# Hybrid decoder block: parameter loads as rows, and the gates of the second token block made when that block begins

## The chip, the cores and the metric

One core of a Trainium2 chip runs the whole program. The metric is the device time of one execution in microseconds (us). The kernel before took 3391.08 us (median of 3 runs, 3389.36 to 3392.07).

## The reference, cut to what matters

A block of 2048 tokens and 1024 channels: two branches in parallel, merged with gates, and then a dense part.

```
h = rms(x);  u, q, k, v, qi, ki, wi, gates = split(h @ w_in)
y_ssm = s5(u, A_re, A_im, log_dt, B, C, D_skip, ...)   # state space scan, gelu, glu
y_att = dsa(q, k, v, qi, ki, wi)                       # the best 256 keys of each query, then softmax
g_ssm, g_att = split(gates)                            # 2 x 1024 columns
merged = sigmoid(g_ssm) * (y_ssm @ w_proj_ssm) + sigmoid(g_att) * (y_att @ w_proj_attn)
x = x + merged @ w_out
x = x + (silu(h2 @ w_gate) * (h2 @ w_up)) @ w_down     # h2 = rms(x), 2816 columns inside
```

All in float32. The matrix products are each made as three products of parts (high by high, high by low, low by high), which the code calls mm3.

## The kernel before, in words

**Who sets the order.** The kernel writes one order of instructions for each engine. It is made by a planner (class Pace) that keeps an estimated clock of each engine: generators yield what they wait for, and the first in the list that is ready by TensorE's estimated clock goes on. The list is state space branch, attention, dense part; so the dense part fills what the two others leave free. All loads and stores are issued by SyncE (SP) in one queue, in order.

**Phase 1** (names tp, mm, hT, w, raw) norms x, transposes it into hT and multiplies it with the columns of w_in for keys, queries and u. The state space parameters are prepared beside it (`ssm_params`): its loads and small VectorE operations are put into a queue, `small`, of which `drain` takes up to 8 after each tile of q or u. In the queue all loads stand first: A_re, A_im, log_dt and D_skip are read straight into a layout with state and group on the partitions, in pieces of one element; B_re and B_im in pieces of 16 elements.

**Gates** (`gates`, names gps, gw, gsg): 16 column tiles of 128 for each half of the tokens, the second half first. Each weight tile is loaded raw and split into a high and a low part by GpSimd (POOL), VectorE (DVE) or ScalarE (ACT); a gate is 24 matmuls of 512 columns, a tanh on ACT, and a store. For the first half, hT is read back from the tensor hTd, which phase 1 stores. Tokens 0 to 511 are block 0 of the dense part, tokens 512 to 1023 block 1.

**Attention** goes over four groups of four query tiles. Each has scores of the indexer (tps), a search of the thresholds (`topk`: counting on DVE, names jkd, tr, un, cnt, and on ACT, jka), and then the attention itself (lg, pt, po). The search needs little of TensorE.

**Dense part** (`block`, PSUM name f) for four token blocks of 512: merge (f<-act,ww, one load of a gate tile and one product on DVE for each bank), w_out (f<-ww,mg), norm, and the feed-forward: up and gate (f<-h,ww) and down (f<-wd,at, where each 6 matmuls end in one addition x<-f,x on DVE). In block 0 each weight is loaded raw, split, and its parts stored (wc<-ww); the later blocks load the parts. Block 0 begins when the glu of the state space branch is done (name u) and the gates are; each later block when the attention of its group is.

Of the kernel before, what the change touches and what calls it, by code (L numbers as in the profile page):

```python
# [25 lines left out]
KD = D // 128  # L26
# [25 lines left out]
class Pace:  # L52
# [95 lines left out]
    def at(self, eng, *what):  # L148

        return lambda: self.when(eng, what) + (None,)  # L150
# [215 lines left out]
class Block:  # L366
    def __init__(self, ctx, tc, a, out):
        self.tc, self.a, self.out = tc, a, out
        self.pace = self.nc = nc = Pace(tc.nc)
        self.const = self.pool(ctx, "const", 1)  # L370
        self.attended, self.act, self.gated, self.exps = 0, [], False, False
        self.spare_banks, self.lent = 0, False
        self.dram = ctx.enter_context(tc.tile_pool(name="scr", bufs=1, space=DRAM))
        c = self.const
        self.ident = c.tile([128, 128], F32, name="ident")
        make_identity(tc.nc, self.ident)
        self.mhalf = c.tile([128, 64], F32, name="mhalf")
# [12 lines left out]
        self.u_d = [d.tile([128, G, TC, PG], F32, name=f"u{i}") for i in range(2)]  # L390
        self.hT_d = d.tile([128, 2, KD, HALF], F32, name="hTd")
        self.bias_d = [d.tile([128, (i + 1) * 128], BF16, name=f"bias{i}") for i in range(NT)]
        self.gate_d = [[d.tile([128, HALF], F32, name=f"gate{j}_{h}") for h in range(2)] for j in range(2 * KD)]
        self.y_d = [[d.tile([64, HALF], F32, name=f"y{i}_{h}") for h in range(2)] for i in range(8)]
        self.act_d, self.att_d = ([d.tile([128, 2, 4, TB], F32, name=f"{n}{i}") for i in range(NB)]
                                  for n in ("act", "att"))
# [338 lines left out]
    def gates(self, hT, st):  # L735
# [21 lines left out]
            yield  # L757
        psp = self.pool(st, "gps", 2, PSUM)
        NG = 2 * KD
        order = [(n, tg) for n in range(2 * NG) for tg in range(2)]  # L760

        order[2 * NG - 4:2 * NG + 4] = [(NG + n, tg) for n0 in (-2, 0) for tg in range(2) for n in (n0, n0 + 1)]
        there = [[0.0, 0.0], [0.0, 0.0]]
        parts = deque()

# [7 lines left out]
        left = [2] * (2 * NG)  # L773
        for q, (n, tg) in enumerate(order):
            hf, ct = 1 - n // NG, n % NG
            ld.need(2 * n + 2)
            ld.allowed = 2 * sum(z == 0 for z in left) + 4
            left[n] -= 1
            w = tiles[n]
            sl = slice(tg * 512, (tg + 1) * 512)  # L780
            while parts and parts[0][0] == tg:
                reload()
            yield self.pace.at("PE", w, there[tg][0], psp.free_at("gps"))
            if q in (2 * NG - 2, 2 * NG):
                parts.extend((q - 2 * NG + 2 >> 1, h, i) for h in range(2) for i in range(2))
# [444 lines left out]
    def ssm_params(self, pr, wk, ps_t, queue):  # L1230

        nc, a = self.nc, self.a
        NS = G // 2
        dv, sync, cmul = Later(queue, nc.vector), Later(queue, nc.sync), self.cmul
        sh = [128, NS]
        A = {}
        for n in ("A_re", "A_im"):
            A[n] = wk.tile(sh, F32, name=n)
            ap = a[n]
            sync.dma_start(A[n], bass.AP(tensor=ap.tensor, offset=ap.offset, ap=[[1, 128], [128, NS]]))  # L1240
        dt = wk.tile(sh, F32, name="dt")
        ap = a["log_dt"]
        for g2 in range(2):
            sync.dma_start(dt[g2 * 64:(g2 + 1) * 64],
                              bass.AP(tensor=ap.tensor, offset=ap.offset + g2, ap=[[0, 64], [2, NS]]))
        Ds = pr.tile([32, NS], F32, name="Ds")
        ap = a["D_skip"]
        sync.dma_start(Ds, bass.AP(tensor=ap.tensor, offset=ap.offset, ap=[[1, 32], [32, NS]]))
        B, C, turns = [], [], []
        for n in ("B_re", "B_im"):  # L1250
            t = wk.tile([128, NS, PG], F32, name=n)
            ap = a[n]
            sync.dma_start(t, bass.AP(tensor=ap.tensor, offset=ap.offset,
                                         ap=[[PG, 128], [128 * PG, NS], [1, PG]]))
            B.append(t)
        for n in ("C_re", "C_im"):
            t = pr.tile([128, NS, PG], F32, name=n)
            ap = a[n]
# [14 lines left out]
        ar, ai = A["A_re"], A["A_im"]  # L1273
# [55 lines left out]
        u1, u2 = (wk.tile([128, NS, PG], F32, name=f"u{n}") for n in "12")  # L1329
# [5 lines left out]
        dv.tensor_tensor(eye, self.ident[:32, 0:PG], self.ident[:32, PG:2 * PG], op=ALU.add)  # L1335
        queue.extend(turns)
        return m8, ap_r, ap_i, wt, Bb, C, eye, Ds

# [302 lines left out]
    def weights(self):  # L1641
# [23 lines left out]
        return [(kind, parts, copy, tb > 0) for tb in range(NB) for (kind, parts), copy in zip(items, copies)]  # L1665

    def load_branch(self, bigp, br, tb):

        z = bigp.tile([128, 2, 4, TB], F32R, name=f"act{br}")
        for k in range(4):  # L1670
            self.nc.sync.dma_start(z[:, :, k].bitcast(F32), (self.act_d, self.att_d)[br][tb][:, :, k])
        return z

    def block(self, tb, bigp, ld, nps, nd):

# [7 lines left out]
        with ExitStack() as st:  # L1683
# [25 lines left out]
            def ready(*w):  # L1709
                return at("PE", free, *w)  # L1710

            with ExitStack() as sm:
                mp = self.pool(sm, "mg", 1)
                mg = mp.tile([128, 2, KD, n], F32R, name="mg")
                with ExitStack() as sp:
# [9 lines left out]
                    load_gate(0, 0)  # L1725
# [3 lines left out]
                    load_gate(1, 0)  # L1729
                    load_gate(0, 1)  # L1730
                    load_gate(1, 1)
                    for q, (ct, br) in enumerate([(0, 0), (1, 0), (0, 1), (1, 1)] +
                                                 [(ct, br) for ct in range(2, KD) for br in range(2)]):
# [9 lines left out]
                        if br == 1:  # L1743
# [172 lines left out]
                        yield from down(pairs.popleft(), False)  # L1916
                pairs.append(acts)
            if tb + 1 < NB:
                self.act = [self.load_branch(bigp, br, tb + 1) for br in range(1 + (self.attended >= 4 * (tb + 2)))]
# [83 lines left out]
```

## Time and profile before

| | |
|---|---|
| median of the runs | 3391.08 us |
| the profiled execution's own time | 3392.47 us |
| its span | 3390.8 us |
| PE busy | 3179.1 us (94%) |
| DVE busy | 2118.4 us (62%) |
| ACT, POOL busy | 1277.2 us (38%), 622.4 us (18%) |
| DMA | 605.67 MB, 51.1% of 16 engines |

Read it by stages: the shares are means over stages with different limits. A row of the timeline gives the start, the duration of a run of like instructions, the engine, and in brackets the idle time before it and what ended it. Matmuls are pipelined, so a PE that is busy all the time can still be slow: what counts is how many of them are done in a stretch.

### The profile page before, as it was taken

What the parts mean: (1) busy time and instruction counts of PE and PEld (TensorE: products, weight loads), DVE (VectorE), ACT (ScalarE), POOL (GpSimd) and SP (SyncE); (2) the same over time, 40 slices, a digit from 0 to 9 for tenths busy, and PEclk for the clock granted to TensorE, in tenths of its full rate; (3) what the DMA queues carried; (4) which work ended last, traced back from release to release, by engine and by line L of the source; (5) the groups of instructions that cost most, each with busy time, mean ns of one, the idle gap of its engine ahead of it and who ended that gap; (6) DMA issues with size and microseconds to landing.
All of it is one profiled execution on the core that took longest, in us unless ns stands there. A gap on an engine that the chain in (4) does not pass through costs nothing. (4 is left out here: it accounts for less than half of the span.)

```text
span 3390.8 us, 44218 instructions
## 1 busy us (share of the span) xinstructions
PE 3179.1 (94%) x16292; PEld 2687.4 (79%) x16292; DVE 2118.4 (62%) x4540; ACT 1277.2 (38%) x2210; POOL 622.4 (18%) x620
## 2 busy tenths in 40 slices
PE   6999999899878999988889999999999999899999
PEld 5889777677767888876788888878888888698887
DVE  5565595655687767689686675867776666322223
ACT  3141444445552444355412443666124443010000
POOL 3323666522233212134100000000000000000000
PEclk8999999999989999999999999999999999999999
DMA  4834423434458766656845324376472332755554
GB/s 135 249 119 116 132 77 121 153 123 142 130 174 293 271 210 231 238 175 236 310 152 218 146 105 165 123 259 229 166 271 99 114 133 103 271 193 201 204 199 161
DMA packets 321527, 605.67 MB, mean 179 GB/s; under 512 B 52896, under 2 KB 205216, under 8 KB 290592
## 3 DMA queue, kind: packets, MB, share of 16 engines
q1 hardware_dynamic: 321312, 602.86, 51.1%
q8 instruction: 128, 2.10, 0.2%
q14 instruction: 87, 0.71, 0.1%
HBM read 434.71 MB, written 166.89 MB: 177 GB/s over the span
## 5 line engine op out<-in xcount | busy, mean ns | idle before, releaser
L206 PE MATMUL f<-h,ww 128*128 128x512 f32 (+1 forms) x4416 | 1015.0, 384 | 1.4 <-DVE h L206 1.1
L206 PEld LDWEIGHTS f<-h,ww 128*128 128x128 f32 x4416 | 800.6, 190 | 156.4 <-DVE h L206 1.9
L206 PE MATMUL f<-wd,at 128*128 128x512 f32 x2112 | 521.1, 399 | 42.8 <-DVE un L206 16.0
L206 PEld LDWEIGHTS f<-wd,at 128*128 128x128 f32 x2112 | 398.5, 192 | 133.3 <-DVE x L206 13.6
L206 PE MATMUL gps<-hT,gw 128*128 128x512 f32 x1536 | 386.5, 402 | 5.2 <-ACT gsg L206 3.7
L206 ACT ACTIVATE jka<-S,tr 128x1536 bf16<-128x1536 f32 (+5 forms) x217 | 305.6, 1408 | 193.6 <-DVE tr L206 119.2
L206 PEld LDWEIGHTS gps<-hT,gw 128*128 128x128 f32 x1536 | 287.7, 192 | 70.0 <-ACT gsg L206 6.4
L206 DVE TENSOR_TENSOR x<-f,x 128x512 f32<-128x512 f32 x352 | 236.4, 687 | 103.2 <-PE f L206 102.5
L206 PE MATMUL mm<-w,hT 128*128 128x512 f32 (+1 forms) x1152 | 281.5, 402 | 7.2 <-DVE hT L206 7.0
L206 DVE TENSOR_TENSOR tl<-pt,th 128x512 fp32r<-128x512 f32 (+1 forms) x288 | 184.2, 658 | 135.9 <-ACT th L206 135.1
L206 PEld LDWEIGHTS mm<-w,hT 128*128 128x128 f32 x1152 | 241.8, 241 | 32.6 <-DVE hT L206 8.7
L206 DVE SCALAR_TENSOR_TENSOR t<-t,f 128x512 f32<-128x512 f32 (+1 forms) x125 | 83.5, 668 | 278.5 <-PE f L206 238.0
L206 ACT CAST th<-pt 128x512 fp32r<-128x512 f32 (+1 forms) x288 | 155.8, 563 | 234.1 <-PE pt L206 230.3
L206 PE MATMUL f<-act,ww 128*128 128x512 f32 x768 | 189.9, 408 | 29.7 <-POOL ww L206 9.1
L206 PEld LDWEIGHTS f<-act,ww 128*128 128x128 f32 x768 | 149.2, 197 | 70.3 <-POOL ww L206 13.3
L206 PE MATMUL f<-ww,mg 128*128 128x256 f32 x1536 | 190.4, 287 | 10.8 <-ACT ww L206 4.5
L206 PEld LDWEIGHTS f<-ww,mg 128*128 128x128 f32 x1536 | 188.7, 195 | 12.9 <-ACT ww L206 5.0
L206 ACT ACTIVATE P<-P,m 128x1024 f32<-128x1024 f32 (+7 forms) x192 | 172.3, 900 | 54.5 <-DVE m L206 54.4
L206 POOL TENSOR_TENSOR g<-g,g 128x512 f32<-128x512 f32 x31 | 39.8, 1285 | 813.3 <-DVE g L206 793.5
L206 PE MATMUL lg<-kk,q 128*128 128x512 f32 (+1 forms) x640 | 183.7, 388 | 1.1 <-DMA kk<-kk 1.1
L206 ACT ACTIVATE t<-f 128x512 f32<-128x512 f32 (+1 forms) x92 | 53.0, 576 | 332.9 <-PE f L206 332.7
L206 ACT CAST at<-t 128x512 fp32r<-128x512 f32 (+1 forms) x92 | 55.3, 601 | 324.1 <-DVE t L206 324.1
(359 smaller groups left out, 4492.2 us busy)
## 6 DMA issues: line engine op xcount, KB each, us to landing
ww<-wc SPq DMA_DIRECT2D x180, 1024.0 KB, 4.9
wd<-wc SPq DMA_DIRECT2D x66, 1024.0 KB, 8.3
wc<-ww SPq DMA_DIRECT2D x60, 1024.0 KB, 7.7
raw<-in_w_in_dram SPq DMA_DIRECT2D x104, 256.0 KB, 3.4
wc<-wd SPq DMA_DIRECT2D x22, 1024.0 KB, 7.6
x<-in_x_dram SPq DMA_DIRECT2D x32, 512.0 KB, 5.1
gate<-gsg SPq DMA_DIRECT2D x64, 256.0 KB, 2.2
g<-gate SPq DMA_DIRECT2D x64, 256.0 KB, 5.0
```

What stands on the lines that cost most here:

```text
L206: return f(*args, **kw)
```

## The change

Parameters: A_re, A_im, D_skip and log_dt are loaded as rows (16 partitions), four small transposes on TensorE turn them (`columns`), and ACT copies them out of PSUM. B_re and B_im are loaded in four pieces each, and the loads of B and the rest of C stand between the small operations instead of ahead of all of them. Gates: in the first half of the tokens `gates` makes only tokens 0 to 511, and stores each split weight tile (`gw_d`). Block 1 begins with 16 gate products from these stored parts and from hT, which is loaded from hTd into the buffers of the activations; its branches are loaded as those buffers come free, attention first.

```diff
+        self.late = (1,)
+        self.gw_d = [d.tile([128, 2, 1024], F32, name=f"gw{j}") for j in range(2 * KD)]
...
-        order = [(n, tg) for n in range(2 * NG) for tg in range(2)]
-
-        order[2 * NG - 4:2 * NG + 4] = [(NG + n, tg) for n0 in (-2, 0) for tg in range(2) for n in (n0, n0 + 1)]
+        order = [(n, tg) for n in range(NG) for tg in range(2)] + [(NG + n, 0) for n in range(NG)]
+
+        order[2 * NG - 4:2 * NG] = [(n, tg) for tg in range(2) for n in (NG - 2, NG - 1)]
...
-            if q in (2 * NG - 2, 2 * NG):
-                parts.extend((q - 2 * NG + 2 >> 1, h, i) for h in range(2) for i in range(2))
+            if q == 2 * NG - 2:
+                parts.extend((0, h, i) for h in range(2) for i in range(2))
+            if n >= NG:
+                nc.sync.dma_start(self.gw_d[ct], w.rearrange("p z k c -> p z (k c)").bitcast(F32))
...
+        for z, n, m in ((rows[0], "A_re", 128), (rows[1], "A_im", 128), (d32, "D_skip", 32), (d2, "log_dt", 2)):
+            sync.dma_start(z, bass.AP(tensor=a[n].tensor, offset=a[n].offset, ap=[[m, NS], [1, m]]))
...
+        def columns():
+            nc.scalar.copy(rows[2].rearrange("p (a n) -> p a n", a=2), d2[:, :, None].to_broadcast([NS, 2, NST]))
+            ps = ps_t.tile([128, 512], F32, name="tp")
+            for i, z in enumerate(rows):
+                nc.tensor.transpose(ps[:, i * NS:(i + 1) * NS], z, self.ident[:NS, :NS])
+            nc.tensor.transpose(ps[:32, 3 * NS:4 * NS], d32, self.ident[:NS, :NS])
+            nc.scalar.copy(A.rearrange("p a s -> p (a s)"), ps[:, :3 * NS])
+            nc.scalar.copy(Ds, ps[:32, 3 * NS:4 * NS])
...
-            sync.dma_start(t, bass.AP(tensor=ap.tensor, offset=ap.offset,
-                                         ap=[[PG, 128], [128 * PG, NS], [1, PG]]))
+            for s0 in range(0, NS, 4):
+                sync.dma_start(t[:, s0:s0 + 4], bass.AP(tensor=ap.tensor, offset=ap.offset + s0 * 128 * PG,
+                                                        ap=[[PG, 128], [128 * PG, 4], [1, PG]]))
...
+        queue.extend(head)
+        queue.extend(loads.popleft() for _ in range(24))
+        queue.append(columns)
+        for i, step in enumerate(steps):
+            queue.append(step)
+            if i % 6 == 5 and loads:
+                queue.append(loads.popleft())
...
+                [("w", None, copy, True) for copy in self.gw_d if tb in self.late] +
...
+                    order = list(range(KD))
+                    last = 3
+                    for ct in range(2 * KD - last):
+                        w = ld.get("w")
+                        yield ready(w, *hg)
+                        ps = bank()
+                        yield from products(ps, w, order)
+                        ld.drop("w")
+                        gated(ct, ps)
...
+                    self.act = [None, self.load_branch(bigp, 1, tb)]
+                    for i in range(last):
+                        w = ld.get("w")
+                        yield from products(banks[i], w, order[KD // 2:])
+                        ld.drop("w")
+                        gated(2 * KD - last + i, banks[i])
+                    self.act[0] = self.load_branch(bigp, 0, tb)
...
+                if tb + 1 in self.late:
+                    self.act = self.load_tokens(bigp, tb + 1)
```

The queue of SP in phase 1, from the third weight load on. Before (A, dt, Ds, B and C are the parameters, raw a weight):

```order
L206 DMA raw<-in_w_in_dram 128x512 x3
L206 DMA A_re<-in_A_re_dram 128x16x1
L206 DMA A_im<-in_A_im_dram 128x16x1
L206 DMA dt<-in_log_dt_dram 64x16x1 x2
L206 DMA Ds<-in_D_skip_dram 32x16x1
L206 DMA B_re<-in_B_re_dram 128x16x16
L206 DMA B_im<-in_B_im_dram 128x16x16
L206 DMA C_re_568<-in_C_re_dram 16x2x64
L206 DMA raw<-in_w_in_dram 128x512 x3
```

The same place now (u_577 and u_578 are buffers for the rows):

```order
L206 DMA raw<-in_w_in_dram 128x512 x3
L206 DMA u_577<-in_A_re_dram 16x128
L206 DMA u_577<-in_A_im_dram 16x128
L206 DMA u_578<-in_D_skip_dram 16x32
L206 DMA u_578<-in_log_dt_dram 16x2
L206 DMA C_re_584<-in_C_re_dram 16x2x64 x4
L206 DMA raw<-in_w_in_dram 128x512 x3
```

Between the two groups of weight loads stand eight small loads; the first pieces of B have moved behind the loads of C.

TensorE at the end of the glu (u) and the begin of block 0, before (act_9327 and act_9364 are the two branches):

```order
L206 MATMUL gps<-hT,gw 128x512 x24
L206 MATMUL u<-yp,uw_7369 128x256 x12
L206 MATMUL u<-yp,uw_7374 128x256 x12
L206 MATMUL gps<-hT,gw 128x512 x6
L206 MATMUL u<-yp,uw_7416 128x256 x12
L206 MATMUL u<-yp,uw_7443 128x256 x12
L206 MATMUL gps<-hT,gw 128x512 x330
L206 MATMUL f<-act_9327,ww 128x512 x24
```

and now:

```order
L206 MATMUL gps<-hT,gw 128x512 x24
L206 MATMUL u<-yp,uw_7424 128x256 x12
L206 MATMUL u<-yp,uw_7429 128x256 x12
L206 MATMUL u<-yp,uw_7481 128x256 x12
L206 MATMUL u<-yp,uw_7484 128x256 x12
L206 MATMUL u<-yp,uw_7424 128x256 x12
L206 MATMUL u<-yp,uw_7429 128x256 x12
L206 MATMUL u<-yp,uw_7481 128x256 x12
L206 MATMUL u<-yp,uw_7484 128x256 x12
L206 MATMUL f<-act_8639,ww 128x512 x24
```

The 330 gate matmuls between the glu and block 0 are gone, and the last 96 matmuls of the glu have no gate between them.

TensorE at the end of block 0 and the begin of block 1 now (tps is the indexer of the third group, hg the stored hT, act the branches):

```order
L206 MATMUL tps<-kis,qi 128x512 x8
L206 MATMUL f<-wd,at 128x512 x6
L206 MATMUL tps<-kis,qi 128x256 x8
L206 MATMUL f<-wd,at 128x512 x66
L206 MATMUL f<-hg_13765,ww 128x512 x12
L206 MATMUL f<-hg_13768,ww 128x512 x12
...
L206 MATMUL f<-hg_13768,ww 128x512 x48
L206 MATMUL f<-hg_13765,ww 128x512 x36
L206 MATMUL f<-act_14743,ww 128x512 x24
```

Before, 240 down and 294 up matmuls of block 0 stood between the third group's last tps and the first f<-act of block 1; now 66 down matmuls and the 384 gate matmuls stand there. Where the second group's search runs, between the last u and the first lg of that group, the order of TensorE holds 408 up matmuls of 512 columns and 144 down matmuls behind the merge, w_out and norm of block 0; before it held 330 gate matmuls ahead of them, 108 up matmuls behind, and no down. After the last lg of the program 186 more matmuls of 512 columns are left than before. On POOL, 89 splits of the dense part's weights stand where there were 69.

## Rows read from the trace of the kernel before

**Rows 1.** The page: busy tenths of TensorE in 40 slices of the span.

```profile
PE   6999999899878999988889999999999999899999
```

**Rows 2.** By stretch: length; busy PE, PEld, DVE, ACT, POOL; clock, DMA share, GB/s.

```profile
70.00:80.00 10.00, 0.00 (x0) 0.00 (x0) 0.00 (x0) 0.00 (x0) 0.00 (x0) 0.60 0.05 0
...
900.00:981.00 81.00, 77.17 (x337) 62.02 (x336) 71.76 (x263) 59.55 (x104) 17.21 (x15) 1.00 0.29 88
981.00:1163.00 182.00, 147.07 (x814) 125.87 (x815) 135.05 (x262) 55.04 (x82) 57.48 (x31) 0.90 0.79 278
1478.00:1634.00 156.00, 127.24 (x506) 100.20 (x506) 143.36 (x296) 86.93 (x111) 65.44 (x28) 0.91 0.67 237
```

**Rows 3.** Timeline of SP's issues in phase 1: start, time taken, load.

```profile
56.80 0.42 SPq L206 DMA_DIRECT2D A_re<-in_A_re_dram  x1
57.28 3.56 SPq L206 DMA_DIRECT2D A_im<-in_A_im_dram  x1
...
66.66 4.80 SPq L206 DMA_DIRECT2D B_re<-in_B_re_dram  x1
71.50 12.86 SPq L206 DMA_DIRECT2D B_im<-in_B_im_dram  x1
...
85.81 1.31 SPq L206 DMA_DIRECT2D raw<-in_w_in_dram  x3
```

**Rows 4.** Timeline of the compute engines around the same place.

```profile
61.20 1.04 PE L206 MATMUL tp<-ident,x 128*128 128x128 f32 x8
...
88.70 0.43 DVE L206 CAST w<-raw 128x512 fp32r<-128x512 f32 x1 [23.31 <-DMA raw<-in_w_in_dram]
...
91.74 1.97 PE L206 MATMUL tp<-ident,q 128*128 128x128 f32 x8 [22.15 <-DVE hT L206]
```

**Rows 5.** Timeline of TensorE between the glu and block 0.

```profile
900.66 26.44 PE L206 MATMUL gps<-hT,gw 128*128 128x512 f32 x114
928.71 22.49 PE L206 MATMUL gps<-hT,gw 128*128 128x512 f32 x96 [1.61 <-ACT gsg L206]
952.83 27.96 PE L206 MATMUL gps<-hT,gw 128*128 128x512 f32 x120 [1.64 <-ACT gsg L206]
989.65 5.43 PE L206 MATMUL f<-act,ww 128*128 128x512 f32 x12 [8.86 <-DMA act<-act]
```

**Rows 6.** Timeline of TensorE at the end of block 0, beside the third group's search.

```profile
1497.26 21.93 PE L206 MATMUL f<-h,ww 128*128 128x512 f32 x96
1519.02 1.07 PE L206 MATMUL f<-wd,at 128*128 128x512 f32 x4
...
1543.41 23.47 PE L206 MATMUL f<-h,ww 128*128 128x512 f32 x96
1566.72 1.07 PE L206 MATMUL f<-wd,at 128*128 128x512 f32 x4
...
1583.52 11.04 PE L206 MATMUL f<-h,ww 128*128 128x512 f32 x48
1594.40 1.07 PE L206 MATMUL f<-wd,at 128*128 128x512 f32 x4
...
1632.05 2.11 PE L206 MATMUL f<-act,ww 128*128 128x512 f32 x8 [1.86 <-DVE x L206]
```

**Rows 7.** Timeline of DVE at the begin of that search: the same instruction twice.

```profile
1486.52 2.38 DVE L206 SCALAR_TENSOR_TENSOR tr<-un,tr 128x1 int32<-128x1 int32 x1
...
1491.95 0.16 DVE L206 SCALAR_TENSOR_TENSOR tr<-un,tr 128x1 int32<-128x1 int32 x1
```

**Rows 8.** Groups of instructions: count, busy us, mean ns of one, idle before and releasers.

```profile
L206 DVE TENSOR_TENSOR x<-f,x 128x512 f32<-128x512 f32 x352 | 236.4, 687 | 103.2 <-PE f L206 102.5
...
L206 POOL TENSOR_TENSOR ww<-raw,ww 128x1024 fp32r<-128x1024 f32 x33 | 81.4, 2468 | 110.4 <-ACT ww L206 90.0 <-DVE m L206 7.9 <-DMA wc<-ww 7.7
...
L206 POOL TENSOR_TENSOR ww<-raw,zeros 128x1024 fp32r<-128x1024 f32 x13 | 28.3, 2174 | 79.2 <-PE f L206 38.7 <-DMA raw<-in_w_proj_attn_dram 24.1 <-DMA raw<-in_w_ffn_gate_dram 11.4
```

**Rows 9.** Timeline of TensorE where the fourth group's attention has ended and block 2 ends.

```profile
2908.60 1.62 PE L206 MATMUL f<-wd,at 128*128 128x512 f32 x3 [5.36 <-DMA wd<-wc]
```

More of the change, by code (lines that the diff above doesn't have):

```diff
@@ L771, in reload @@
                 there[tg][h] = self.pace.ready(hT)
-        left = [2] * (2 * NG)
+        left = [2] * NG + [1] * NG
         for q, (n, tg) in enumerate(order):
@@ L1233, in ssm_params @@
         NS = G // 2
-        dv, sync, cmul = Later(queue, nc.vector), Later(queue, nc.sync), self.cmul
+        head, steps, loads = [], [], deque()
+        dv, cmul = Later(steps, nc.vector), self.cmul
         sh = [128, NS]
[L1236 to L1245, printed above, removed]
-        Ds = pr.tile([32, NS], F32, name="Ds")
-        ap = a["D_skip"]
-        sync.dma_start(Ds, bass.AP(tensor=ap.tensor, offset=ap.offset, ap=[[1, 32], [32, NS]]))
+        u1, u2 = (wk.tile([128, NS, PG], F32, name=f"u{n}") for n in "12")
+        v1, v2 = (u.rearrange("p s c -> p (s c)")[:NS] for u in (u1, u2))
+        rows = [v1[:, 0:128], v1[:, 128:256], v2[:, 0:128]]
+        d32, d2 = v2[:, 128:160], v2[:, 160:162]
+        sync = Later(head, nc.sync)
+        for z, n, m in ((rows[0], "A_re", 128), (rows[1], "A_im", 128), (d32, "D_skip", 32), (d2, "log_dt", 2)):
+            sync.dma_start(z, bass.AP(tensor=a[n].tensor, offset=a[n].offset, ap=[[m, NS], [1, m]]))
+        A = wk.tile([128, 3, NS], F32, name="A")
+        Ds = pr.tile([32, NS], F32, name="Ds")
+        def columns():
[6 more added lines that the diff above has]
+            nc.scalar.copy(Ds, ps[:32, 3 * NS:4 * NS])
+        dt = A[:, 2]
+        late = []
+        sync = Later(late, nc.sync)
         B, C, turns = [], [], []
@@ L1252, in ssm_params @@
             ap = a[n]
[L1253 to L1254 removed]
+            for s0 in range(0, NS, 4):
+                sync.dma_start(t[:, s0:s0 + 4], bass.AP(tensor=ap.tensor, offset=ap.offset + s0 * 128 * PG,
+                                                        ap=[[PG, 128], [128 * PG, 4], [1, PG]]))
             B.append(t)
+        sync = Later(loads, nc.sync)
         for n in ("C_re", "C_im"):
@@ L1272, in ssm_params @@
             C.append(t)
-        ar, ai = A["A_re"], A["A_im"]
+        ar, ai = A[:, 0], A[:, 1]
         edt, _ = self.exp_parts(dv, dt, wk, sh, "ed")
@@ L1335, in ssm_params @@
         dv.tensor_tensor(eye, self.ident[:32, 0:PG], self.ident[:32, PG:2 * PG], op=ALU.add)
+        loads.extend(late)
+        queue.extend(head)
[5 more added lines that the diff above has]
+                queue.append(loads.popleft())
+        assert not loads and len(steps) > 7 * 16
         queue.extend(turns)
@@ L1664, in weights @@
         copies = [self.dram.tile([128, 2, 1024], F32, name=f"wc{i}") for i in range(len(items))]
-        return [(kind, parts, copy, tb > 0) for tb in range(NB) for (kind, parts), copy in zip(items, copies)]
+        return [z for tb in range(NB) for z in
+                [("w", None, copy, True) for copy in self.gw_d if tb in self.late] +
+                [(kind, parts, copy, tb > 0) for (kind, parts), copy in zip(items, copies)]]
     def load_branch(self, bigp, br, tb):
@@ L1672, in load_branch, with load_tokens @@
         return z
+    def load_tokens(self, bigp, tb):
+        hg = []
+        for i in range(2):
+            ks = slice(i * KD // 2, (i + 1) * KD // 2)
+            hg.append(bigp.tile([128, 2, KD // 2, TB], F32R, name=f"hg{i}", tag=f"act{i}"))
+            for z in range(2):
+                self.nc.sync.dma_start(hg[i][:, z].bitcast(F32), self.hT_d[:, z, ks, tb * TB:(tb + 1) * TB])
+        return hg
     def block(self, tb, bigp, ld, nps, nd):
@@ L1710, in ready, with products, gated @@
                 return at("PE", free, *w)
+            b0 = 0
+            if tb in self.late:
+                b0 = 1
+                with ExitStack() as sg:
+                    gp = self.pool(sg, "lsg", 2)
+                    hg = self.act
+                    def products(ps, w, ks):
+                        w = w.rearrange("p z a (k c) -> p (z a) k c", k=KD)
+                        for k in ks:
+                            z = hg[k // 4]
+                            self.mm3(ps, w[:, 0, k], w[:, 1, k], z[:, 0, k % 4], z[:, 1, k % 4], k == order[0],
+                                     k == order[-1])
+                            if k % 2 == 1:
+                                ld.tick()
+                                if k != order[-1]:
+                                    yield at("PE")
+                    def gated(ct, ps):
+                        g = gp.tile([128, n], F32, name="lg")
+                        nc.scalar.activation(g, ps, AF.Tanh, scale=0.5)
+                        nc.sync.dma_start(self.gate_d[ct][hf][:, h0:h0 + n], g)
+                    order = list(range(KD))
[7 more added lines that the diff above has]
+                        gated(ct, ps)
+                    order = [*range(KD // 2, KD), *range(KD // 2)]
+                    banks = []
+                    for i in range(last):
+                        w = ld.get("w", i)
+                        yield ready(w)
+                        banks.append(bank(False))
+                        yield from products(banks[i], w, order[:KD // 2])
+                    self.act = [None, self.load_branch(bigp, 1, tb)]
+                    for i in range(last):
+                        w = ld.get("w")
[3 more added lines that the diff above has]
+                    self.act[0] = self.load_branch(bigp, 0, tb)
             with ExitStack() as sm:
@@ L1728, in block @@
                     self.act = []
[L1729 to L1733, printed above, removed]
+                    load_gate(1, b0)
+                    load_gate(0, b1)
+                    load_gate(1, b1)
+                    for q, (ct, br) in enumerate([(0, b0), (1, b0), (0, b1), (1, b1)] +
+                                                 [(ct, br) for ct in range(2, KD) for br in (b0, b1)]):
                         w = ld.get("w", 1 if q == 1 else 0)
@@ L1918, in block @@
             if tb + 1 < NB:
-                self.act = [self.load_branch(bigp, br, tb + 1) for br in range(1 + (self.attended >= 4 * (tb + 2)))]
+                if tb + 1 in self.late:
+                    self.act = self.load_tokens(bigp, tb + 1)
+                else:
+                    self.act = [self.load_branch(bigp, br, tb + 1)
+                                for br in range(1 + (self.attended >= 4 * (tb + 2)))]
             yield from down(pairs.popleft(), False)
```

6 lines of the change are left out of this document (3 added, 3 removed).

## The prediction

> **What bounds the kernel now.** I read the busy tenths of TensorE first [rows 1]: it is busy nearly everywhere, so its work is the floor, and what can be gained is the time in which it stands or gets through few matmuls. The change neither adds nor removes products of size: 384 gate matmuls go from one place to another. So I looked for the stretches in which TensorE loses time, and asked which of them the moved work touches. Three matter.
>
> The first is in phase 1. SyncE needs 3.56 us to issue A_im and 12.86 us for B_im, against 0.42 us for A_re, which I read as the many small pieces of the loads ahead filling the queue; the next weight loads are issued only at 85.81 [rows 3]. DVE then waited 23.31 us for them, and TensorE stood for 22.15 us [rows 4]. From 70 to 80 no compute engine did anything [rows 2], so nothing was done ahead in that time.
>
> The second is where the second attention group's search runs, from the end of the glu at about 900 to 1163. First 330 gate matmuls cover it, at nearly full rate: PE is busy 77.17 of 81 us [rows 2, 5]. Then block 0 begins, and PE is busy only 147.07 of 182 us.
>
> The third is the third group's search, 1478 to 1634: 506 matmuls of 512 columns in 156 us [rows 2]. At the full rate, 21.93 us for 96 or 0.228 us for one [rows 6], they need 115.6 us, so 40 us are lost. The loss is in the down parts: every 6 matmuls wait for an addition of 0.687 us on DVE [rows 8], which is busy 143.36 of the 156 us. DVE itself is held up while POOL splits weights: the same one-element instruction takes 2.38 us there and 0.16 us a little later [rows 7].
>
> **The change, part by part.** *The parameter loads.* In place of A, dt, Ds and B stand eight loads, each of a few hundred pieces at most. At the 0.42 us of A_re [rows 3] they take 3.4 us of SyncE, so that the next weights are issued at about 60 and not at 85.81. A weight reached DVE 2.9 us after that issue (88.70 less 85.81) [rows 3, 4], so it is there at about 63, and DVE asked for it at 65.4 (88.70 less 23.31). The stall of 22.15 us goes. With it goes the slow start behind it, 1.97 us for eight transposes that took 1.04 us before [rows 4]. Against these 23 us stand four small transposes and three ACT copies, about 1 us. I take -22 us. What may be late next are the eight pieces of B: they are issued between weights later. From below, they cost nothing, since the weights are loaded ahead; from above, a quarter of B_im's 12.86 us each, 25.7 us in all, which would eat the gain.
>
> *The gates that go.* The 330 gate matmuls between the glu and block 0 took from 900.66 to 980.79, 80.1 us, for 75.3 us of work at 0.228 us. Their other 54 stood between the matmuls of the glu and filled its waits. Of the work nothing is saved; the 5 us that they lost there go: -5 us. The glu's last 96 matmuls have no filler now, which costs at most 54 times 0.228, 12 us; since without a filler in the way they can follow each other faster, I take 0.
>
> *Block 0 comes 80 us earlier and lies wholly in the second group's search.* Its start (8.86 us of waiting for the branch [rows 5]) and its merge lose what they lost before. New there are 144 down matmuls, three parts of 48, which the order now has ahead of that group's first lg. The nearest rows are the down parts in the third group's search [rows 6]: 1519.02 to 1543.41 is 24.4 us for 48, 1566.72 to 1583.52 is 16.8 us, 1594.40 to 1632.05 is 37.7 us for 96. Less 11.0 us of work for 48 that is a loss of 13.4, 5.8 and twice 7.9 us, 8.7 us in the mean: +26 us for three, from 0 if that search has ended by then to +40 at the worst part. The second cost is POOL's: 20 more splits, 2.17 or 2.47 us each [rows 8], stand on it, at most 49 us in which DVE's search may stand. DVE was busy 71.76 and 135.05 of the 263 us [rows 2], so 56 us are free, and the additions and products that come in take some 17 us of them (24 additions of 0.687 us; what the up parts bring to DVE is about what it saves in splits). The rest hides most of it; I take +7, from 0 to +49. Together +33 us.
>
> *Block 1 begins with the gates.* They need DVE for nothing: tanh on ACT, a store, and weights that are already split. In the third group's search the 240 down matmuls become 66, and no POOL split is left beside it. Of the 40 us lost I keep 66/48 of 8.7 us, 12 us. The gates themselves read 4 MB of hT and 1 MB of weights for each 24 matmuls, and then the two branches come into buffers that the gates have just left. The nearest row is the wait of 8.86 us for a branch at block 0's start [rows 5]; between 0 and twice that I take +7. So -40 + 12 + 7 = -21 us, from -40 to -4.
>
> *The tail.* With less work beside the searches at the end, the attention of the last group ends earlier: 186 more matmuls follow its last lg. The loads of block 2's end and block 3's start no longer meet its loads; the wait of 5.36 us [rows 9] may go. I take -4, from -9 to 0.
>
> The stores of the 16 weight tiles, 1 MB each, lie beside the attention of the first group and the glu. I take nothing for them: the DMA share was 0.29 between 900 and 981 [rows 2], and it must triple before it binds.
>
> **The sum.** -22 - 5 + 33 - 21 - 4 = -19 us on the profiled execution's 3392.47 us (span 3390.8), that is 3373 us; the median of the runs is 1.4 us below that execution, so 3372 us.
>
> **The rivals.** *The moved work costs the second search nothing.* The planner may have spread the down parts such that DVE keeps up. For it: DVE had 56 us to spare there. Against it: DVE was just as far from full in the third search's longer stretch, and the down parts lost all the same. Then the +33 falls away: 3339 us.
>
> *POOL and DVE block each other in the second search, and the kernel gets slower.* Place: block 0 with POOL's splits beside the counting of the second group, which till now ran beside gates and 17.21 us of POOL in 81 [rows 2]. A DVE instruction that meets a split waits for it [rows 7]. If all 49 us of new splits are on the path and each down part costs the worst 13.4 us, the +33 becomes +89, and the sum +37: 3428 us. It decides against the change from the point where block 0's place costs over 52 us. The Trainium skill (SBUF — State Buffer, section SBUF: two separate sides) calls the port that the two share an exclusive lock: the loser stands for the whole instruction. The 2.38 us against 0.16 us [rows 7] agree, about as long as one split; by that rule every split would count in full where DVE has work, which is this rival.
>
> *The stall only moves.* B still comes in 64 byte pieces, as many as before; if each of the eight pieces holds up SyncE by its quarter of 12.86 us [rows 3] just before a weight, the 22 us are lost again, and the sum is about +2: 3394 us. The Trainium skill (DMA: Bandwidth & Descriptors, section Specifications) wants at least 512 bytes in a transfer for full rate, which the rows of A now have and B has not. Against the rival: the stall took A, dt, Ds and B in one go, and now weights stand between the pieces.
>
> **How the numbers follow.** Forecast 3372 us, 0.50, with its own range of 3355 to 3389. Second search free: 3339 us, 0.16. POOL and DVE: 3428 us as its worst case, from 3400 on, 0.16. Stall moves: 3394 us, 0.12. The remaining 0.06 lies between them. Half of the second case lies below 3337, and most of the third above 3403; with about 0.2 left out, the range is 3337 to 3403. A measurement of this kernel can tell 0.2%, 6.8 us, from no change. Faster by that: 0.47 of the forecast, 0.16, 0.03 of the stall case and 0.05 of the rest, 0.71. Slower: 0.15 of the third case, 0.02 of the stall case, 0.17. The same: 0.12.
>
> **What would show it.** Right, if in the profile after TensorE has no gap over 3 us between 57 and 92; if the glu ends near 878 (900 less 22); if the first lg of the second group comes at about 1194 (878, the 182 us that it took before from the glu's gates to it, 444 more matmuls at 0.228, and 33 us), and the down parts there take 15 to 24 us for 48; if the gate matmuls of block 1 run at 0.23 us one after the other; and if the third group's search stretch loses under 20 us. It is wrong if TensorE stands in phase 1 again, if the first lg of the second group comes after 1220 (the POOL rival) or before 1170 (the free search), or if the first gates of block 1 wait over 10 us for hT.

## The result, and the profile after

The changed kernel takes 3419.66 us (median of 4 runs, 3413.48 to 3424.74) against 3391.57 us before in the same series (4 runs, 3389.36 to 3394.85): ratio 1.0078, 95% interval 1.0063 to 1.0094. It is slower by about 28 us, where 3372 was forecast. The profiled execution took 3417.55 us; its span is 3415.8 us, 25.0 us longer than before.

The page, busy tenths of TensorE in 40 slices, answers to [rows 1]:

```profile
PE   7999989998686899998899999999899999999999
```

The first slice rose by a tenth. The low place in slices 11 to 13 (854 to 1110 us), where block 0 now lies, is deeper: 6, 8, 6 tenths where 8, 7, 8 stood. The stretch of phase 1 in which TensorE was idle for 22 us [rows 4], by the view of stretches (columns as in [rows 2]), and by the timeline of TensorE:

```profile
57.00:92.00 35.00, 30.12 (x152) 25.55 (x151) 22.20 (x43) 13.29 (x29) 17.22 (x14) 0.95 0.55 174
```

The stall is gone. The last matmuls of phase 1 on TensorE, before and after:

```profile
361.03 1.65 PE L206 MATMUL mm<-w,hT 128*128 128x512 f32 x6
```

```profile
345.79 1.65 PE L206 MATMUL mm<-w,hT 128*128 128x512 f32 x6
```

Other places on the way to block 1's merge after the change, from the timeline of TensorE; they answer to [rows 5, 6]:

```profile
82.87 0.31 PE L206 MATMUL tp<-ident,u 16*128 16x16 f32 x2 [3.77 <-ACT u L206]
...
873.13 0.58 PE L206 MATMUL u<-yp,uw 128*128 128x256 f32 x1 [5.44 <-ACT t L206]
874.01 7.70 PE L206 MATMUL u<-yp,uw 128*128 128x256 f32 x47 [0.30 <-DVE yp L206]
891.59 1.22 PE L206 MATMUL f<-act,ww 128*128 128x512 f32 x2 [9.89 <-POOL ww L206]
...
1044.63 1.94 PE L206 MATMUL f<-ident,ha 128*128 128x128 f32 x8 [23.46 <-DVE ss L206]
...
1123.46 0.84 PE L206 MATMUL f<-wd,at 128*128 128x512 f32 x3
...
1139.22 5.39 PE L206 MATMUL f<-wd,at 128*128 128x512 f32 x12 [5.86 <-DVE t L206]
1144.45 21.92 PE L206 MATMUL f<-h,ww 128*128 128x512 f32 x96
1166.21 9.68 PE L206 MATMUL f<-wd,at 128*128 128x512 f32 x42
...
1177.65 21.92 PE L206 MATMUL f<-h,ww 128*128 128x512 f32 x96
1199.41 2.88 PE L206 MATMUL f<-wd,at 128*128 128x512 f32 x12
...
1211.47 5.61 PE L206 MATMUL f<-h,ww 128*128 128x512 f32 x24
...
1216.91 0.89 PE L206 MATMUL lg<-kk,q 128*128 128x512 f32 x4
...
1548.79 12.71 PE L206 MATMUL f<-wd,at 128*128 128x512 f32 x44 [3.78 <-DVE un L206]
1561.33 87.59 PE L206 MATMUL f<-hg,ww 128*128 128x512 f32 x384
1653.83 9.25 PE L206 MATMUL f<-act,ww 128*128 128x512 f32 x27 [4.90 <-DMA ww<-wc]
```

The largest wait is new: 23.46 us ahead of the norm's first transposes in block 0, put down to DVE. The gates of block 1 run without a gap, 87.59 us for 384. What TensorE waited for between the glu's end and block 1's merge (sum of us, times, longest), before, 900 to 1632:

```profile
PE f L206 <- POOL ww L206: 11.1, 8, 2.0
PE f L206 <- DVE un L206: 10.5, 3, 4.9
```

and after, 882 to 1654:

```profile
PE f L206 <- POOL ww L206: 26.8, 12, 9.9
PE f L206 <- DVE ss L206: 23.5, 1, 23.5
```

The direct waits for POOL's parts (ww) rose by 15.7 us; 9.9 of them stand at block 0's start, where before 8.86 us went to the branch [rows 5].

Now DVE itself, from the groups of instructions between 860 and 1240 (count, busy us, mean ns of one, idle before). Before:

```profile
L206 DVE SCALAR_TENSOR_TENSOR tr<-un,tr 128x1 int32<-128x1 int32 (+1 forms) x72 | 23.3, 323 | 2.5
L206 DVE SCALAR_TENSOR_TENSOR jkd<-H,tr,jkd 128x320 bf16<-128x320 bf16 (+1 forms) x30 | 18.9, 629 | 1.1
L206 DVE TENSOR_TENSOR_SCAN S<-ones,fin 128x1024 f32<-128x1024 f32 (+3 forms) x4 | 7.6, 1891 | 0.1
```

After:

```profile
L206 DVE SCALAR_TENSOR_TENSOR tr<-un,tr 128x1 int32<-128x1 int32 (+1 forms) x72 | 35.5, 493 | 2.5
L206 DVE SCALAR_TENSOR_TENSOR jkd<-H,tr,jkd 128x320 bf16<-128x320 bf16 (+1 forms) x30 | 30.9, 1032 | 1.1
L206 DVE TENSOR_TENSOR_SCAN S<-ones,fin 128x1024 f32<-128x1024 f32 (+3 forms) x4 | 16.1, 4026 | 0.1
L206 DVE TENSOR_TENSOR x<-f,x 128x512 f32<-128x512 f32 x24 | 15.3, 683 | 1.4 <-PE f L206 1.4
```

These three groups, the same instructions in the same number, take 82.5 us where they took 49.8; the additions out of PSUM (x<-f,x) cost 683 ns as ever [rows 8]. Not every group rose: two others of the counting (jkd<-H,tf,jkd and jkd<-H,tf) fell from 43.7 to 36.5 us. All instructions of the search together went from 169 us (459 of them) to 219 (456).

When DVE was held matters. The same one-element instruction while w_out runs on TensorE, and during TensorE's wait of 23.46 us:

```profile
1007.08 1.68 DVE L206 SCALAR_TENSOR_TENSOR tr<-un,tr 128x1 int32<-128x1 int32 x1
...
1022.61 0.16 DVE L206 SCALAR_TENSOR_TENSOR tr<-un,tr 128x1 int32<-128x1 int32 x1
```

In the wait itself nothing holds DVE: it works off the search instructions that stand in its queue ahead of the additions which the norm needs. The delay arose before, while w_out ran: POOL made 17 splits there (4 before the change). By an estimate, the length of each DVE instruction less that of the same one in the run without splits on POOL (below), DVE lost 27 us there, and 6 before.

POOL's groups beside them after, from 882 to 1217:

```profile
L206 POOL TENSOR_TENSOR ww<-raw,ww 128x1024 fp32r<-128x1024 f32 x34 | 84.4, 2484 | 60.8 <-ACT ww L206 45.7 <-DVE tr L206 7.8 <-DVE fin L206 4.2
L206 POOL TENSOR_TENSOR ww<-raw,zeros 128x1024 fp32r<-128x1024 f32 x19 | 38.8, 2044 | 72.4 <-DMA raw<-in_w_proj_attn_dram 39.8 <-PE f L206 21.9 <-DMA raw<-in_w_ffn_gate_dram 6.4
```

### The profile page after: what moved, and what is told of

The parts are those of the page before. It is cut to its first block, busy times and chain, and to the rows that moved or that the text cites. A ratio compares the mean times of both kernels' runs of the same rounds, so it can differ in the third digit from the quotient of the medians.

```text
span 3415.8 us, 44290 instructions
## 1 busy us (share of the span) xinstructions
PE 3191.4 (93%) x16296; PEld 2695.4 (79%) x16296; DVE 2122.0 (62%) x4527; ACT 1275.9 (37%) x2215; POOL 657.7 (19%) x631
## 5 line engine op out<-in xcount | busy, mean ns | idle before, releaser
L206 ACT ACTIVATE jka<-S,tr 128x1536 bf16<-128x1536 f32 (+6 forms) x217 | 305.4, 1407 | 183.7 <-DVE tr L206 97.9
L206 PE MATMUL gps<-hT,gw 128*128 128x512 f32 x1152 | 299.0, 407 | 7.0 <-ACT gw L206 3.6
L206 PEld LDWEIGHTS gps<-hT,gw 128*128 128x128 f32 x1152 | 216.1, 194 | 55.2 <-issue 4.4
```

The source lines that it names most:

```text
L206: return f(*args, **kw)
```

## The experiments

My theory after the two profiles: the rows are worth what phase 1 shows, and the gates' move costs some 45 us, because POOL's splits of block 0 now lie beside DVE's search and hold it. The rivals: the second search has lost its cover (gate matmuls, which need nothing of it) and DVE lags for want of it, POOL or not; or only the planner's order is at fault. Medians, and ratios to the kernel before on the same chip (before: 3393 to 3394 us):

| run | us | ratio, 95% interval |
|---|---|---|
| rows alone | 3379.83 | 0.996 [0.9947, 0.9973] |
| late gates alone | 3437.92 | 1.0127 [1.0114, 1.014] |
| changed, search held back during w_out | 3408.08 | 1.0043 [1.0031, 1.0055] |
| changed, half of the late gates | 3413.82 | 1.0063 [1.0051, 1.0075] |
| before, split by ACT alone (copies) | 3371.47 | 0.9935 [0.992, 0.9949] |
| changed, split by ACT alone (copies) | 3349.27 | 0.9872 [0.9859, 0.9885] |
| the same, with idle work on POOL | 3442.03 | 1.0136 [1.0122, 1.015] |
| changed, high ACT, low DVE | 3382.66 | 0.9969 [0.9957, 0.998] |
| rows, high ACT, low DVE | 3376.29 | 0.995 [0.9938, 0.9962] |
| half late, high ACT, low DVE | 3379.6 | 0.9956 [0.9944, 0.9969] |
| rows, high ACT, low by planner | 3394.18 | 0.9999 [0.999, 1.0008] |
| changed, high ACT, low by planner | 3442.34 | 1.0146 [1.013, 1.0161] |
| changed, low DVE, high by planner | 3392.88 | 0.9998 [0.9988, 1.0009] |
| rows, low DVE, high by planner | 3365.67 | 0.9906 [0.989, 0.9923] |

**The two parts apart.** First the new `ssm_params` in the kernel before, then the new gates with the old `ssm_params` (the changed kernel with that function put back); of each edit the first lines:

```diff
-        dv, sync, cmul = Later(queue, nc.vector), Later(queue, nc.sync), self.cmul
+        head, steps, loads = [], [], deque()
+        dv, cmul = Later(steps, nc.vector), self.cmul
...
```

```diff
-        head, steps, loads = [], [], deque()
-        dv, cmul = Later(steps, nc.vector), self.cmul
+        dv, sync, cmul = Later(queue, nc.vector), Later(queue, nc.sync), self.cmul
...
```

> The kernel before with the parameter loads as rows alone; the gates stay where they were. Theory (the stall in phase 1 is really gone, and the gates' move costs what is lost): glu and the gates behind it end 17 to 20 us earlier, block 0 begins at about 970 instead of 989.65, and the time is about 3372 us (0.9945 of before). Rival (what phase 1 gains is lost again at the glu or at the attention, whatever the gates do): within 6 us of before, 3391 us.

> The kernel before with the late gates alone; the parameter loads stay as they were, with their stall of 22 us in phase 1. Theory (the two parts add up, and the gates' move costs 45 us by itself): about 3437 us (1.0135), with a wait of 15 to 25 us before the transposes of block 0's norm. Rival (only the two together hurt, since the glu comes too early for the first attention group): 3391 to 3405 us, norm wait under 10 us.

Measured -14 us (-18 to -9) and +44 us; together +31, against +28 for the whole change. The parts add up within the intervals. The rows gave less than 22: block 0 begins at 978.47 instead of 989.65, 11 us earlier, where 970 was expected. With the gates alone the norm waited 22.63 us, as in the whole change.

**The order alone.**

```diff
+                self.pace.tight = tb == 0
                 for cg in range(D // NC):
```

> The changed kernel, with one planner rule moved: in block 0 the search of the second group is held back to DVE's estimated clock (the rule that so far holds only for the first four banks of the merge and for the last of w_out) from the start of w_out to the end of the norm. Theory (the norm of block 0 waits because about 135 search instructions stand between the eight additions of w_out in DVE's order): the wait of 23.46 us on ss falls under 8 us; the search ends later by some of it; time 3400 to 3408 us. Rival (DVE is slow because POOL's splits hold it, whatever the order): the wait stays above 15 us, or as much is lost before the first lg, and the time is within 5 us of 3420.

TensorE's timeline in this run:

```profile
1025.76 1.06 PE L206 MATMUL f<-ident,ha 128*128 128x128 f32 x8 [1.97 <-DVE ss L206]
...
1116.89 12.10 PE L206 MATMUL f<-wd,at 128*128 128x512 f32 x44 [10.21 <-DVE wd L206]
```

The norm's wait is gone, but 10.21 us of it stand at the next place that needs DVE. The time falls by 11.6 us, just at the expectation's edge: the order chose where the wait stood, and explains at most these 12 us of what the gates cost.

**Half of the gates.**

```diff
-        order = [(n, tg) for n in range(NG) for tg in range(2)] + [(NG + n, 0) for n in range(NG)]
...
+        order = [(n, tg) for n in range(NG + KD) for tg in range(2)] + [(NG + KD + n, 0) for n in range(KD)]
...
-        left = [2] * NG + [1] * NG
+        left = [2] * (NG + KD) + [1] * KD
...
```

> The changed kernel with half of the late gates: of the 16 for tokens 512 to 1023 the 8 of the state space branch are made early, as before, and the 8 of the attention branch when block 1 begins. Theory (each late gate takes cover from the second search, and the cost grows with their number): -19 us for the rows and about half of +45 for the gates, 3390 to 3396 us; block 0 begins at about 930. Rival (the first few late gates are free, since DVE has room): 3372 us or less. Second rival (any late gate brings the norm under the search): 3415 us or more.

3413.82 us: against the rows alone, half of the gates cost 34 us, and all 40; the intervals of the two overlap, so the step from half to all is not clear of noise. TensorE's timeline:

```profile
1086.80 1.94 PE L206 MATMUL f<-ident,ha 128*128 128x128 f32 x8 [13.06 <-DVE ss L206]
```

The theory of a cost per gate misses by 18 us. The run is nearer to the second rival, whose 3415 it just fails to reach.

**No splits on POOL.** In `Loader.split`, for block 0's weights:

```diff
+        if isinstance(self, Rings):
+            p.scalar.copy(hi, raw)
+            p.scalar.copy(lo, raw)
+            self.fill()
+            return
```

Both kernels leave out the low parts: a second copy of the weight stands in their place.

> The kernel before, with block 0's weights split by ACT alone: the high part is its copy, and in place of the low part stands a second copy (so the low parts are not those of the reference). POOL and DVE make no split in block 0. To be compared with the next run. Both theories: 3375 to 3395 us, since block 0's waits for POOL's low parts shorten, and ACT gets 74 copies of about 1.04 us more.

> The changed kernel with the same: block 0's weights split by ACT alone, a second copy in place of the low part (so the low parts are not those of the reference). Theory (the move costs because POOL's splits hold DVE's search; in the second search tr<-un,tr takes 502 ns in the mean after and 335 before, the scan 4026 and 1891): without POOL's splits tr falls to about 0.16 us and the scan to 1.9, the norm's wait of 23.46 us shrinks below 6, and the difference to the run before this one shrinks from +28 to between -20 and +5 us. Rival (the second search has lost its cover of gates, and DVE would lag with or without POOL): the difference stays at +15 to +35 us.

The kernel before falls to 3371 us, below the 3375 expected. The difference between the two kernels turns from +28 to -22 us, just past the theory's -20. DVE in the second run, between 860 and 1240:

```profile
L206 DVE SCALAR_TENSOR_TENSOR jkd<-H,tr,jkd 128x320 bf16<-128x320 bf16 (+1 forms) x30 | 17.5, 584 | 1.1
L206 DVE SCALAR_TENSOR_TENSOR tr<-un,tr 128x1 int32<-128x1 int32 (+1 forms) x72 | 12.9, 179 | 2.5
L206 DVE TENSOR_TENSOR_SCAN S<-ones,fin 128x1024 f32<-128x1024 f32 (+3 forms) x4 | 7.6, 1891 | 0.1
```

38.0 us for what took 82.5, with block 0 just as much beside the search, and TensorE's wait at the norm is 2.80 us. The gates' cover was not needed; the splits were what it hid. But these runs take DVE's own splits away too (8 of 1.22 us in the changed kernel), and TensorE's direct waits for POOL. So next the hold alone: the same order of everything else, and beside each split one subtraction on POOL that nobody waits for.

```diff
+            p.scalar.copy(hi, raw)
+            p.scalar.copy(lo, raw)
+            p.gpsimd.eng.tensor_tensor(self.b.idle_tile, self.b.idle_tile, self.b.idle_tile, op=ALU.subtract)
...
```

> The changed kernel with ACT alone splitting (a second copy in place of the low part, so the low parts are not those of the reference; 3349 us in its run), and beside each split one POOL subtraction of 128x1024 on a tile that nothing else reads. The planner does not know of it, so the order of all other instructions is that of the run without it. Theory (a POOL instruction of this size holds DVE by itself, though nobody waits for its result): tr<-un,tr in the second search rises from 179 to 350 ns or more, the scan from 1891 to above 2500, and the time by 25 to 50 us, to 3375 to 3400 us. Rival (what cost was TensorE waiting for low parts made by POOL): within 8 us of 3349. The four rr of the norm, which are on POOL, may come up to 2.5 us later each in both.

3442.03 us, 93 us more, nearly twice the upper expectation. POOL's timeline in this run, and then DVE's:

```profile
1058.17 67.05 POOL L270 TENSOR_TENSOR idle<-idle 128x1024 f32<-128x1024 f32 x33
```

```profile
1078.72 1.73 DVE L206 TENSOR_SCALAR uf<-cnt 128x2 f32<-128x2 f32 x1
1080.49 0.16 DVE L206 SCALAR_TENSOR_TENSOR tf<-uf,tf 128x2 f32<-128x2 f32 x1
1080.68 1.82 DVE L206 TENSOR_SCALAR jkd<-H,tf 128x320 bf16<-128x320 uint16 x1
1082.54 2.18 DVE L206 SCALAR_TENSOR_TENSOR jkd<-H,tf,jkd 128x320 bf16<-128x320 uint16 x1
1084.66 0.07 DVE L206 DVE_READ_ACCUMULATOR jkd<-H,tf,jkd 128x1 f32 x1
...
1119.34 0.41 DVE L206 SCALAR_TENSOR_TENSOR t<-t,f 128x256 f32<-128x256 f32 x1
```

POOL goes on without a gap, 2.03 us each, and most DVE instructions last until about the next of POOL's ends. Behind them a product that TensorE needed (t<-t,f, itself 0.41 us) came so late that TensorE stood for 49 us:

```profile
1123.21 18.05 PE L206 MATMUL f<-h,ww 128*128 128x512 f32 x72 [49.09 <-ACT ww L206]
```

The releaser named is ACT; its copies were queued behind one that waited 56 us for that t:

```profile
1119.78 0.41 ACT L206 CAST at<-t 128x256 fp32r<-128x256 f32 x1 [56.46 <-DVE t L206]
```

No wait of TensorE between 882 and 1217 names POOL. tr and the scan rose less than expected (277 and 2284 ns, for 350 and 2500), the counting more (jkd<-H,tf,jkd 585 to 1244 ns): which instructions are hit depends on when POOL works. As a whole the search answers to POOL's work beside it: its instructions take 129 us without splits, 196 in the run with half of the late gates, 219 in the changed kernel with 61 splits (141 us of POOL), and 213 here with 72 idle subtractions (145 us).

**The whole computation without POOL's splits.** High parts on ACT, low parts on DVE:

```diff
+        if isinstance(self, Rings):
+            p.scalar.copy(hi, raw)
+            p.vector.tensor_tensor(lo, raw, hi.bitcast(F32), op=ALU.subtract)
+            self.fill()
+            return
```

> The changed kernel; in block 0 every high part is made by ACT and every low part by DVE (1.22 us each, in the trace), none by POOL. Theory (a split on POOL costs DVE about as much as doing it itself, and the planner does not know it): DVE's search instructions are as short as before, the wait for the norm falls, and the time is 3395 to 3410 us. Rival (DVE is simply full, and 34 more splits of 1.22 us make it worse): 3420 us or more.

> The kernel before with the parameter rows (3380 us), and with the high parts of block 0 on ACT and the low ones on DVE. Theory: here fewer splits stand beside the search (17 of POOL from 981 to 1163 in the kernel before), so less is to be had: 3365 to 3380 us, and if it is below 3375, faster than both kernels. Rival (DVE full): 3385 us or more.

> Half of the late gates (3414 us by itself) with high parts on ACT and low parts on DVE. Theory (with POOL out of the way the place of the gates hardly matters): 3372 to 3386 us, between the rows with DVE's low parts (3376) and all gates late with them (3383). Rival (the late gates cost by themselves, whoever splits): above 3395 us.

The changed kernel gains 37 us, 12 more than the theory's best; with the rows alone only 4, which is not clear of noise. With POOL out, no late, half late and all late gates take 3376, 3380 and 3383 us, where with POOL they take 3380, 3414 and 3420. The place of the gates hardly matters then, but it is no gain either, probably because DVE has the low parts to make: with copies by ACT alone the late gates did gain.

**Only one of the two kinds of split off POOL.** First the high parts on ACT, the low ones where the planner puts them; then the reverse:

```diff
-        eng = p.spare(hi, ("POOL", "DVE", "ACT"))
+        eng = p.scalar if isinstance(self, Rings) else p.spare(hi, ("POOL", "DVE", "ACT"))
```

```diff
-        p.spare(lo).tensor_tensor(lo, raw, hi.bitcast(F32), op=ALU.subtract)
+        e = p.vector if isinstance(self, Rings) else p.spare(lo)
+        e.tensor_tensor(lo, raw, hi.bitcast(F32), op=ALU.subtract)
```

> The parameter rows alone, with block 0's high parts on ACT and the low parts where the planner puts them (POOL or DVE). Theory: between 3380 (rows alone) and 3376 (low parts on DVE), or a little under both, since TensorE no longer waits for POOL's high parts: 3370 to 3380 us. Rival (ACT's 1.04 us each delays the second search's counting): above 3383 us.

> The changed kernel with the high parts of block 0 on ACT and the low parts where the planner puts them. A dose between the changed kernel (3420 us, 58 POOL splits between 890 and 1217) and the one without splits on POOL (3383 us): without the 21 high parts 34 to 40 remain. Theory: 3392 to 3408 us. Rival (the low parts alone do the harm, since a subtraction reads two operands): 3412 us or more.

> The changed kernel; in block 0 the low parts are made by DVE, and the high parts by POOL, ACT or DVE as the planner chooses. Theory (the subtractions on POOL do the harm: 2.5 us each, they hold DVE, and TensorE waits for them behind ACT's copy): near the run without splits on POOL, 3378 to 3395 us. Rival (any POOL instruction of this size beside the search does): 3405 us or more.

> The parameter rows alone (gates early); block 0's low parts on DVE, the high parts as the planner chooses. Theory: at or under the run with high parts on ACT (3376 us), since TensorE waits less for ACT: 3366 to 3378 us, the fastest correct version so far. Rival (any POOL instruction does harm): above 3385 us.

The first pair fails the theory: 14 us slower than the rows alone and 23 slower than the changed kernel, so that by their numbers both rivals hold. DVE in the changed kernel's version, between 860 and 1240:

```profile
L206 DVE SCALAR_TENSOR_TENSOR tr<-un,tr 128x1 int32<-128x1 int32 (+1 forms) x72 | 20.4, 284 | 2.5
L206 DVE TENSOR_TENSOR_SCAN S<-ones,fin 128x1024 f32<-128x1024 f32 (+3 forms) x4 | 7.6, 1892 | 0.1
```

So the second search is held far less there (158 us for all its instructions), and the loss lies elsewhere. What TensorE waited for in it, 881 to 1670:

```profile
PE f L206 <- ACT ww L206: 21.9, 7, 8.6
PE f L206 <- POOL ww L206: 18.7, 14, 2.3
PE f L206 <- ACT wd L206: 13.8, 3, 7.0
```

ACT's copy and POOL's subtraction now follow each other for each weight, and TensorE waits for both; whether that is the whole of the 23 us stays open. The rows' version points the same way, and against ACT delaying the second search: that group's first lg comes at 1150.5 us, with the rows alone at 1152.0. Its loss comes later, beside the third search (block 1's merge at 1643 instead of 1623), where TensorE's waits for the down weights' parts (wd, from ACT and POOL) rose from 5 to 26 us. So there are two costs of a split on POOL: it holds DVE, and TensorE may wait for it directly. The second pair came out in the theory's range or just below it: 3393 and 3366 us. Taking the subtractions off POOL pays in these orders, moving only the high parts does not. The rows with early gates and DVE's low parts make the fastest kernel that leaves nothing out: 3365.67 us, 26 to 37 us below before by the interval, faster than both kernels. Each of these edits changes the planner's order too, so they are no clean dose.

## Why the prediction was wrong

The steps of the sum, with what they measured between the same places (the span grew by 25.0 us; the forecast of -19 misses by 44):

| step | forecast | measured |
|---|---|---|
| parameter loads, to the end of phase 1 | -22 | -15 |
| the glu without its filler | 0 | +9 |
| gates that go | -5 | -5 |
| block 0 in the second search | +33 | +52 |
| block 1 begins with the gates | -21 | -15 |
| tail | -4 | -1 |

Every step but one came out dearer than forecast. Block 0 is the largest miss, 19 of the 44 us; even with its cost known the sum would have been 0, and the other 25 us are the loads (7), the glu (9), block 1 (6) and the tail (3).

**Parameter loads: right in place, too large by a third.** The stall went; one new wait of 3.77 us came where the transposes' input is copied by ACT (the forecast said no gap over 3). Phase 1's last matmuls start at 345.79 instead of 361.03, 15 us earlier. Alone, the rows were worth 14.

**The glu's filler: taken as 0, it cost 9 of its 12 us.** I said the 54 matmuls would not be missed, since the glu would run faster without them; then I put its end at 878, which is 900 less 22 and leaves no such gain. By 881.7 (874.01 and 7.70) the glu is done, 19 us before the 900.66 of [rows 5]: the 15 of phase 1, and only 4 for 12.3 us of matmuls less. In their place the glu waited for ACT (5.44 us at 873.13).

**Block 0 in the second search: the step that failed.** From 881.7 to 1216.91 are 335.2 us. Less the 181.9 of before (980.79 to 1162.66) and the 444 matmuls more (101.2), that is +52, where the forecast was +33. Its +26 for the down parts was too much: they took 21.0, 11.4 and 12.1 us, a loss of 11.5. Its +7 for POOL was far too little, and it stood in the wrong place. I argued that DVE had 56 us free, and that this would hide most of 49. But the splits held DVE up: the search's instructions took 50 us more, 33 of them in the three groups shown, and DVE lost 27 us to holds while w_out ran, 21 more than before. What it did late was the norm: from w_out's end to the up part's start TensorE took 40.0 us (1021.2 to 1061.2) instead of 13.8, +26; the first up part cost +10, with waits of 1.70 us for POOL's low parts in it, and w_out +4. No step of mine had the norm in it. I counted a free share of DVE over the stretch, and not which instruction of TensorE's path stood behind the search in DVE's queue. That the splits are the cause is borne out by the pair of runs without them: there the difference between the kernels is -22 us, near the -19 forecast, though for kernels without low parts and without DVE's splits.

**Block 1 begins with the gates: right in mechanism, 6 us short.** From the first lg of that group to the gates 344.4 us plus the 101.2 moved ahead make 445.6 against 469.4, -24 (forecast -28). The gates ran at 0.228 us, with no wait for hT. Behind them the weights' load waited 4.90 us and the merge was 12 us longer, w_out and norm shorter: +9, forecast +7.

**The rivals.** "POOL and DVE block each other" (0.16) is what happened by its mechanism: the kernel got slower, and block 0 cost +52, the point from which I said the rival decides. That its 3428 us came within 9 of the result is in part luck: its +89 for block 0 was 52, and the down parts lost 11.5 and not 40; the difference was made up by steps in which it shared the forecast's errors. Its sign in the profile, the second group's first lg after 1220, was missed by 3 us (1216.91). The 2.38 against 0.16 us of [rows 7] was the right row, and I gave it 7 of 49 us. The Trainium skill (SBUF — State Buffer, section Who interferes with whom) says whom it hits: DVE instructions with two inputs in SBUF, or in its two-port modes; with one input in SBUF and outside those modes they go free. The traces agree: the counting, tr and the scan were held, and x<-f,x, which takes one input from PSUM, was not (11 of its 24 lay beside a split and took no longer). In which mode an instruction ran, no row shows. "The stall only moves" (whose sum of "about +2" is +3 by its own terms) is refuted by the run with the rows alone, and "costs nothing" by block 0's +52.

## What to carry to other kernels

Before moving work beside a stretch in which another engine is busy, ask which of its instructions share a resource with that engine, and price each at its full length there; a free share of the engine over the stretch hides nothing if the engine's queue has a critical instruction at its end. A planner that keeps one clock for each engine cannot see one engine hold another, so its best free engine may be the dearest. And two changes in one edit are worth timing apart: here the good one (-14) was buried under the bad one (+44).

## What the runs showed of the hardware

A POOL subtraction of 128x1024 (2.03 us in the idle work, 2.48 in the splits) holds DVE instructions as small as one or two elements per partition: uf<-cnt (two) took 1.73 us beside the idle work and 0.17 with POOL quiet; tr (one) took up to 2.33 in the changed kernel and 0.16 unheld. While POOL ran without a gap, DVE got through about one held instruction for each of POOL's (five in 10.2 us). Reading out an accumulator (0.08 us) and x<-f,x (0.66 to 0.69 us in all 24) were not held. The four scans, 1.89 us in the mean without a split beside them, were each held in the changed kernel, 4.03 us. And 93 us were lost to POOL work whose result nobody read.
